# Two-layer hybrid trunk: one PSUM pool, FFN norm inside the first up product, operands in two passes, the attention's end reordered

## The chip, the cores and the metric

The kernel runs on one core of a Trainium2 chip. Its engines are TensorE (PE, with its weight loads as PEld), VectorE (DVE), ScalarE (ACT), GpSimd (POOL) and SyncE (SP, which issues most DMAs). The metric is device time in microseconds, lower is better. PSUM has eight banks of 128 x 512 float32, into which PE writes and from which DVE and ACT read.

## The reference

The model is a trunk of two pre-norm layers over 16 meta tokens and 512 tokens, width 1024. Layer 0 mixes tokens by causal pooling over windows of 2, 4, 8 and 16, layer 1 by stick-breaking attention with 16 heads of 64. A dense SwiGLU FFN with 2816 hidden units follows each, and a final RMSNorm stands at the end; only the 512 tokens are put out.

```python
def rmsnorm(x, g):
    y = xf * lax.rsqrt(jnp.mean(xf * xf, axis=-1, keepdims=True) + EPS)
    return (y * g.astype(jnp.float32)).astype(x.dtype)

def swiglu(h, w_gate, w_up, w_down):
    return (jax.nn.silu(h @ w_gate) * (h @ w_up)) @ w_down

def _sb_attend(qs, qpos, kvs, kpos):
    z = jnp.einsum('bqhd,bkhd->bhqk', q, k).astype(jnp.float32) * (HEAD_DIM ** -0.5)
    log_keep = jnp.where(mask, jax.nn.log_sigmoid(-z), 0.0)
    later = lax.cumsum(log_keep, axis=3, reverse=True) - log_keep
    a = jnp.where(mask, jnp.exp(jax.nn.log_sigmoid(z) + later), 0.0)
    return jnp.einsum('bhqk,bkhd->bqhd', a.astype(v.dtype), v)
```

## The kernel before

The residual stream lies transposed in SBUF as eight chunks `h0` to `h7` of 128 channels by 528 positions (`hT`). Every float32 product is made of three products of split numbers (`mm3`): high by high, low by high, high by low. ACT writes the high part (a cast), DVE the low part (a subtraction); `wsplit` (L92, L97) does so for weights, whose raw tiles come by DMA on SP's queue.

`Norm.chunk` is run on each chunk of the residual once it is final. It writes the chunk times the gain, split (`uh`, `ul`, L152 and L153), squares it (L157) and adds it to a running sum (L161; the last chunk's add is L128). The products start from these unscaled operands. `norm_bcast` later multiplies the sum by a matrix of ones on PE (L173: `fb0p`, `fb1p` for the FFNs, `abp` for the attention), and ACT and DVE make 1/rms of it (`rstd_of`, L135 to L139), by which the products' results are scaled (L364, L519).

An FFN has 22 hidden blocks of 128, in rounds of 2 and then 4. The first three (`plain`) take 24 products each for gate and up (48 in the first FFN, which works on two halves of 264). The other 19 (`strassen`) make gate and up of both halves of the positions in seven products of 12 steps each; for these `operands` builds seven split operands `xh`, `xl` of four slots each, in four passes of one slot: two scaled chunks `xn` (L381), four differences (L387), seven casts (L389) and seven subtractions (L390), all 264 or 256 wide. It runs after block 0, when 1/rms is there. Three accumulators `pa`, `pb`, `pc` hold the seven products; ACT copies parts of them (L412) and DVE combines them (L430 to L436). While a round's blocks are computed, the down products of the round before (`pd`, L304 and L337) run between them. In the second FFN the down products go to `hn`, with the positions on the partitions.

The attention works on eight pairs of heads. For a pair, `proj` makes q, k and v (`pj`), `Scores` the scores in three groups (`z_832`, `z_0`, `z_416`), each read by ACT as two sigmoids (`kp`, `sg`, L576). Then DVE runs a scan over `kp` (L581) and multiplies `sg` by it (L583), once per head. `turned` transposes the weights on PE (`t`, L594 and L607) and splits them (`a1..h`, `a1..l`, L614 and L616; `a`, L619), and `attend` multiplies them with v (`po`, L633). Output products `wo` (`pw`) of the pairs 0 and 1, 2 to 4, and 5 to 7 add into the residual (L660), in eight steps of six, nine and nine products. Those of 2 to 4 are spread over the last two pairs as filling; those of 5 to 7 end the attention.

A scheduler orders the instructions of each engine from the program, and `tc.issue_after` puts an instruction behind a marked one. In the attention `begin` uses it for the three groups and the steps between them; other steps are placed freely. PSUM is divided anew in each stage by `phase` (L63): `ps0` with eight banks for the pooling, `ps1` with six and two for the first FFN, `ps2` with four and two double ones for the attention, `ps3` as `ps1`. A pool is closed before the next opens. The lines given are those of the kernel before.

## Time and profile before

| what | value |
|---|---|
| runs | 1235.87, 1058.43, 1060.87 us; median 1060.87 |
| profiled execution | 1062.8 us, span 1061.0 us, mean granted clock 0.985 |
| PE busy | 1023.1 us (96%) |
| DVE busy | 856.6 us (81%) |
| ACT busy | 556.9 us (52%) |

The program has these stages, in us of the span: pooling to 37, first FFN 39 to 408, attention 408 to 691, second FFN 695 to 1053, and the last store. A row of the timeline gives start, length, engine, line, operation, output and inputs with buffer numbers left out, shape, and in brackets the idle time before it and what ended it. An overlap of pipelined products makes a row longer than the distance from one start to the next; that distance is what a product takes. A granted clock of 0.5 is TensorE at half speed.

### The profile page before, as it was taken

How to read it: one execution, taken by the hardware profiler on the slowest of the kernel's cores; microseconds unless marked ns; L12 is line 12 of the kernel's file. 1: busy time of each engine (PE TensorE's matmuls, PEld its weight loads, DVE VectorE, ACT ScalarE, POOL GpSimd, SP SyncE). 2: the span in 40 equal slices, each digit the busy share in tenths (PEclk: the TensorE clock that was granted, in tenths of full speed). 3: DMA queues.
4: the chain of work that ended last, by engine and by line, in shares of the span. 5: the costliest groups of instructions: out<-in, count | busy, mean ns of one | idle time of the engine just before them, and what ended most of it. 6: DMA issues, size and time to landing. Idle time of an engine off the chain costs nothing.

```text
span 1061.0 us, 18586 instructions
## 1 busy us (share of the span) xinstructions
PE 1023.1 (96%) x7302; PEld 949.3 (89%) x7302; DVE 856.6 (81%) x1529; ACT 556.9 (52%) x1131; POOL 6.2 (1%) x16
## 2 busy tenths in 40 slices
PE   8998999999999999999999998989999999999997
PEld 6997999999999998998888886867899999999985
DVE  7899987888878777678888987779977877788755
ACT  7555645454444455455555454555655444455544
POOL 1000000000000010000000000000000000000000
PEclk9999999999999999999999998989999999999999
DMA  9212323333333332211111211211223223333302
GB/s 351 72 51 69 128 94 100 101 100 100 100 100 100 99 120 82 78 40 61 40 51 37 69 58 66 80 62 58 100 100 115 84 100 99 100 100 120 109 31 80
DMA packets 43112, 95.73 MB, mean 90 GB/s; under 512 B 3328, under 2 KB 20096, under 8 KB 43024
## 3 DMA queue, kind: packets, MB, share of 16 engines
q1 hardware_dynamic: 42272, 93.40, 26.2%
q8 instruction: 57, 0.93, 0.3%
q10 hardware_dynamic: 752, 1.14, 0.3%
q14 instruction: 31, 0.25, 0.1%
HBM read 92.43 MB, written 2.10 MB: 89 GB/s over the span
## 4 chain that ended last, share of the span: by engine, by line
PE 78%; DVE 17%; issue 2%; ACT 1%; DMA 1%; SPq 0%; ACTq 0%; DVEq 0%
PE pb L106 15%; PE pd L106 11%; PE pd L331 11%; PE pa L106 10%; PE pc L106 10%; PE pj L106 9%; PE pp L106 4%; DVE kp L581 2%; PE pw L106 2%; PE z L567 2%; DVE xl L390 1%; DVE a L619 1%; PE t L594 1%; DVE t L387 1%; DVE sg L583 1%
## 5 line engine op out<-in xcount | busy, mean ns | idle before, releaser
L304 DVE TENSOR_TENSOR h<-pd,h 128x264 f32<-128x264 f32 x96 | 40.9, 427 | 14.0 <-PE pd L106 14.0
L92 ACT CAST ws_3h<-rgate 128x512 fp32r<-128x512 f32 x38 | 23.6, 620 | 53.3 <-PE pb L106 47.8
L581 DVE TENSOR_TENSOR_SCAN kp<-kp,estrip 128x1344 f32<-128x1344 f32 x16 | 47.3, 2954 | 3.8 <-ACT kp L576 3.4
L92 ACT CAST ws_4h<-s 128x512 fp32r<-128x512 f32 x38 | 23.6, 621 | 46.6 <-PE pa L106 27.7
L92 ACT CAST ws_5h<-s 128x512 fp32r<-128x512 f32 x38 | 23.6, 621 | 45.8 <-PE pb L106 34.7
L433 DVE TENSOR_TENSOR u<-pb,m 128x264 f32<-128x264 f32 (+1 forms) x38 | 16.3, 428 | 38.6 <-PE pb L106 38.6
L106 PE MATMUL pa<-xl,ws_0h 128*128 128x264 f32 (+1 forms) x152 | 43.3, 285 | 3.1 <-DVE xl L390 3.0
L106 PE MATMUL pb<-xl,ws_1h 128*128 128x264 f32 (+1 forms) x152 | 43.3, 285 | 1.0 <-DVE xl L390 1.0
L106 PE MATMUL pc<-xl,ws_2h 128*128 128x264 f32 (+1 forms) x152 | 43.1, 283 | 0.9 <-DVE xl L390 0.9
L106 PE MATMUL pb<-xh,ws_1h 128*128 128x264 f32 (+1 forms) x152 | 43.6, 287 | 0.2 <-ACT xh L389 0.2
L106 PE MATMUL pa<-xh,ws_3h 128*128 128x264 f32 (+1 forms) x152 | 43.6, 287 | 0.0
L106 PE MATMUL pa<-xl,ws_3h 128*128 128x264 f32 (+1 forms) x152 | 43.5, 286 | 0.0
L106 PE MATMUL pa<-xh,ws_3l 128*128 128x264 f32 (+1 forms) x152 | 43.3, 285 | 0.0
L106 PE MATMUL pc<-xh,ws_2l 128*128 128x264 f32 (+1 forms) x152 | 43.2, 284 | 0.0
L106 PE MATMUL pa<-xh,ws_0h 128*128 128x264 f32 (+1 forms) x152 | 43.1, 284 | 0.0
L106 PE MATMUL pb<-xh,ws_6l 128*128 128x264 f32 (+1 forms) x152 | 43.0, 283 | 0.0
L106 PE MATMUL pa<-xh,ws_0l 128*128 128x264 f32 (+1 forms) x152 | 43.0, 283 | 0.0
L106 PE MATMUL pb<-xh,ws_4l 128*128 128x264 f32 (+1 forms) x152 | 43.0, 283 | 0.0
L106 PE MATMUL pc<-xl,ws_5h 128*128 128x264 f32 (+1 forms) x152 | 42.9, 283 | 0.0
L106 PE MATMUL pb<-xh,ws_1l 128*128 128x264 f32 (+1 forms) x152 | 42.9, 283 | 0.0
L106 PE MATMUL pb<-xl,ws_4h 128*128 128x264 f32 (+1 forms) x152 | 42.9, 282 | 0.0
L106 PE MATMUL pc<-xh,ws_5h 128*128 128x264 f32 (+1 forms) x152 | 42.9, 282 | 0.0
(1179 smaller groups left out, 4110.9 us busy)
## 6 DMA issues: line engine op xcount, KB each, us to landing
rgate<-in_ffn_w_gate_dram SPq DMA_DIRECT2D x44, 512.0 KB, 3.5
rup<-in_ffn_w_up_dram SPq DMA_DIRECT2D x44, 512.0 KB, 3.5
rd<-in_ffn_w_down_dram SPq DMA_DIRECT2D x42, 512.0 KB, 3.6
rq<-in_sb_w_qkv_dram SPq DMA_DIRECT2D x8, 512.0 KB, 3.5
rk<-in_sb_w_qkv_dram SPq DMA_DIRECT2D x8, 512.0 KB, 3.4
rv<-in_sb_w_qkv_dram SPq DMA_DIRECT2D x8, 512.0 KB, 3.4
rwo<-in_sb_w_o_dram SPq DMA_DIRECT2D x8, 384.0 KB, 3.0
h<-in_x_t_dram SPq DMA_DIRECT2D x8, 264.0 KB, 6.9
```

Source lines behind the costliest of these rows:

```text
L92: nc.scalar.copy(hi, v[:, j:j + w])
L106: last = nc.tensor.matmul(o, lhsT=w, rhs=xx[:, sl], start=start and i == 0, stop=stop and i == 2, skip_group_check=more)
L304: nc.vector.tensor_tensor(out=hv, in0=pd, in1=hv, op=ALU.add)
L331: nc.tensor.matmul(pd, lhsT=hid[j][x_][:, ts], rhs=w_[:, sl], start=r > 0 and i + j == 0, stop=j == len(hid) - 1 and i == 2, skip_group_ch ...
L387: nc.vector.tensor_tensor(out=o, in0=a, in1=b, op=ALU.subtract)
L390: nc.vector.tensor_tensor(out=xl[i][:, m, :], in0=o, in1=f32(xh[i][:, m, :]), op=ALU.subtract)
L433: tt(out=u[:, a], in0=pb, in1=m1, op=ALU.add)
L567: nc.tensor.matmul(tz[:, hd, c:c + k1 - k0], lhsT=qq[hs, i * P:(i + 1) * P], rhs=kk[hs, k0:k1], start=j == 0 and c == 0, stop=False, skip_ ...
L581: nc.vector.tensor_tensor_scan(kp[:, hd, ::-1], kp[:, hd, ::-1], estrip[:, ::-1], 1.0, op0=ALU.mult, op1=ALU.max)
L583: return nc.vector.tensor_tensor(out=sg[:, hd, 0:STRIP - 1], in0=sg[:, hd, 0:STRIP - 1], in1=kp[:, hd, 1:STRIP], op=ALU.mult).ins
L594: nc.tensor.transpose(o, sg[:, c0:c0 + n], ident)
L619: nc.vector.scalar_tensor_tensor(a0[r, i], f32(a0h[r]), lo_rows[r], p2[r, 256:384], op0=ALU.mult, op1=ALU.add)
```

## The change

PSUM becomes one pool for the whole kernel: two double banks (`two`) and two banks each of `c` and `d`. `ps` hands out `one` as c and d in turn, `any` over all eight; `ps_pair` gives the plain blocks theirs. No pool closes any more. In the blocks of Strassen's scheme `pa` and `pb` share one double bank (`pab`), and their copies share tiles `ma`, `mb`.

The ones product of an FFN's norm stands inside block 0's up product, behind its fifth of eight steps (`FB = 4`), and the weights of blocks 1 and 2 are split behind the norm's sum and behind 1/rms. `operands` takes two passes of two slots, so that its differences, casts and subtractions are twice as wide; DVE has 44 instructions fewer in the program and ACT 28. Silu is taken in place.

In the attention every PE step goes through `queued`, which puts it behind the step before. Ahead of the last pair's scores no output product stands; one lies between its groups and three behind them. At the end, `begun` and `ended` divide each output step of the pairs 5 to 7: the products of pairs 5 and 6 of chunk c+1 stand ahead of that of pair 7 of chunk c, and the norm's chunk work follows each.

```diff
+FB = 4
...
-    @contextmanager
-    def phase(name, **bufs):
-        with tc.tile_pool(name=name, bufs=1, space=bass.MemoryType.PSUM) as pool:
-            psum["pool"], psum["bufs"] = pool, bufs
-            yield
+    psum = ctx.enter_context(tc.tile_pool(name="psum", bufs=1, space=bass.MemoryType.PSUM))
+    turn = {"one": 0, "any": 0, "pair": 0}
 
     def ps(name, tag, banks=1):
 
+        i = turn.get(tag, 0)
+        turn[tag] = i + 1
+        if tag == "any":
+            if i % 8 in (0, 1, 4, 5):
+                if i % 2 == 0:
+                    turn["tile"] = ps(name, "two", 2)
+                return turn["tile"][:, i % 2]
+            tag = "cd"[i % 2]
+        if tag == "one":
+            tag = "cd"[i % 2]
         shape = [P, 512] if banks == 1 else [P, banks, 512]
-        return psum["pool"].tile(shape, F32, tag=tag, name=name, bufs=psum["bufs"][tag])
+        return psum.tile(shape, F32, tag=tag, name=name, bufs=2)
+    def ps_pair(name):
+        i = turn["pair"]
+        turn["pair"] = i + 1
+        if i % 3 == 2:
+            return [ps(f"{name}{j}", "c") for j in range(2)]
+        pt = ps(name, "two", 2)
+        return [pt[:, 0], pt[:, 1]]
...
-                add_eps(self.acc, sq, self.acc)
+                self.done = add_eps(self.acc, sq, self.acc)
...
-                parts = [wsplit(raw_gu(kind, f), f"w{kind}{f}") for kind in ("gate", "up")]
-                g, sg, u = (gw(f"{i}{f}") for i in ("g", "sg", "u"))
-                for dst, (wh, wl) in zip((g, u), parts):
-                    pts = [ps(f"pp{f}", "w")[:, :sl.stop - sl.start] for sl in pieces]
+                parts = []
+                for kind in ("gate", "up"):
+                    with tc.issue_after(norm.done if f == 1 else fst[1]) if f else nullcontext():
+                        parts.append(wsplit(raw_gu(kind, f), f"w{kind}{f}"))
+                g, u = (gw(f"{i}{f}") for i in "gu")
+                prods = []
+                both = ps_pair(f"pp{f}") if not full else None
+                for i, (dst, (wh, wl)) in enumerate(zip((g, u), parts)):
+                    pts = [t[:, :sl.stop - sl.start] for t, sl in
+                           zip(ps_pair(f"pp{f}") if full else both[i:i + 1], pieces)]
+                    prods.append((dst, pts))
+                    mark = None
                     for k in range(KC):
-                        mm3([(t, slice(t0 + sl.start, t0 + sl.stop)) for t, sl in zip(pts, pieces)], wh[k], wl[k],
-                            uh[k], ul[k], k == 0, k == KC - 1)
-                    if not fst:
-                        fst.extend((norm_bcast([acc], f"fb{layer}", "d"), last_rstd[0]))
+                        with tc.issue_after(mark) if mark else nullcontext():
+                            last = mm3([(t, slice(t0 + sl.start, t0 + sl.stop)) for t, sl in zip(pts, pieces)], wh[k],
+                                       wl[k], uh[k], ul[k], k == 0, k == KC - 1)
+                        if i == 1 and k == FB and not fst:
+                            with tc.issue_after(last):
+                                fst.extend((norm_bcast([acc], f"fb{layer}", "d"), last_rstd[0]))
+                            mark = last_bcast[0]
...
-                for m in range(4):
+                for m in (0, 2):
                     xn = []
                     for c in (m, m + 4):
-                        t = fp.tile([P, L], F32, tag="xn", name=f"xn{c}", bufs=2)
-                        gc = gains[:, gcol + c:gcol + c + 1]
-                        nc.vector.scalar_tensor_tensor(t[:, tok], hT[c][:, tok], gc, rb[:, tok], op0=ALU.mult,
-                                                       op1=ALU.mult)
+                        t = fp.tile([P, 2, L], F32, tag="xn", name=f"xn{c}", bufs=2)
+                        for j in range(2):
+                            gc = gains[:, gcol + c + j:gcol + c + j + 1]
+                            nc.vector.scalar_tensor_tensor(t[:, j, tok], hT[c + j][:, tok], gc, rb[:, tok],
+                                                           op0=ALU.mult, op1=ALU.mult)
                         xn.append(t)
-                    b11, b12, b21, b22 = [t[:, s] for t in xn for s in halves]
+                    b11, b12, b21, b22 = [t[:, :, s] for t in xn for s in halves]
                     t1, t2, t3, t4 = [wk(f"t{i}") for i in range(4)]
                     for o, a, b in ((t1, b12, b11), (t2, b22, t1), (t3, b22, b12), (t4, b21, t2)):
                         nc.vector.tensor_tensor(out=o, in0=a, in1=b, op=ALU.subtract)
                     for i, o in enumerate((b11, t2, t1, b21, t3, b22, t4)):
-                        nc.scalar.copy(xh[i][:, m, :], o)
-                        nc.vector.tensor_tensor(out=xl[i][:, m, :], in0=o, in1=f32(xh[i][:, m, :]), op=ALU.subtract)
+                        hi, lo = xh[i][:, m:m + 2, :], xl[i][:, m:m + 2, :]
+                        nc.scalar.copy(hi, o)
+                        nc.vector.tensor_tensor(out=lo, in0=o, in1=f32(hi), op=ALU.subtract)
...
-                pa, pb, pc = [ps(f"p{i}{f}", "w")[:, :n] for i in "abc"]
+                pab = ps(f"pab{f}", "two", 2)
+                pa, pb, pc = pab[:, 0, :n], pab[:, 1, :n], ps(f"pc{f}", "c")[:, :n]
...
+                ma, mb = wk(f"ma{f}"), wk(f"mb{f}")
+                m1, m6, m5, m67 = ma[:, 0], ma[:, 1], mb[:, 0], mb[:, 1]
...
-    with phase("ps1", w=6, d=2):
-        ffn(0, 16, norm, before_attention)
-    with tc.tile_pool(name="att", bufs=1) as ap, phase("ps2", one=4, two=2):
...
+        pos = []
+        def queue():
+            return tc.issue_after(pos[0]) if pos else nullcontext()
+        def queued(*steps):
+            for st in steps:
+                with queue():
+                    pos[:] = [st()]
...
-            mark = None
-            for st in before:
-                mark = st()
-            with tc.issue_after(mark) if mark else nullcontext():
-                sc.group(0)
-                mark = sc.group(1)
-            for st in between:
-                with tc.issue_after(mark):
-                    mark = st()
-            with tc.issue_after(mark):
-                sc.group(2)
+            queued(*before, lambda: (sc.group(0), sc.group(1))[1], *between, lambda: sc.group(2))
...
-                fill = w[0:1], w[1:2], w[2:4]
+                fill = [], w[0:1], w[1:4]
...
-            for st in fill[2]:
-                st()
-            attend(p, 1, w1, v, of)
+            queued(*fill[2], lambda: attend(p, 1, w1, v, of))
             if p in (4, 5):
-                for st in early[4 * (p - 4):4 * (p - 3)]:
-                    st()
+                queued(*early[4 * (p - 4):4 * (p - 3)])
...
-        for c, st in enumerate(wo(5, NP)):
-            st()
+        raw, part = [], {}
+        def begun(c):
+            if c % 2 == 0:
+                raw[:] = [wraw(w_o[0, 5 * P:NP * P, c * P:(c + 2) * P].rearrange("(k p) f -> p k f", p=P), f"rwo5_{c}")]
+            ws = wsplit(raw[0][:, :, (c % 2) * P:(c % 2 + 1) * P], f"wo5_{c}")
+            pj = ps(f"pw5_{c}", "one")
+            part[c] = pj, ws
+            for j in range(2):
+                last = mm3([(pj, slice(0, SEQ))], ws[0][j], ws[1][j], *osp[5 + j], j == 0, False)
+            return last
+        def ended(c):
+            pj, ws = part[c]
+            last = mm3([(pj, slice(0, SEQ))], ws[0][2], ws[1][2], *osp[7], False, True)
+            nc.vector.tensor_tensor(out=hT[c][:, TOK], in0=pj, in1=hT[c][:, TOK], op=ALU.add)
             norms[1].chunk(c)
+            return last
+        queued(lambda: begun(0))
+        for c in range(KC):
+            queued(*([lambda: begun(c + 1)] if c + 1 < KC else []), lambda: ended(c))
...
-    ctx.enter_context(phase("ps3", w=6, d=2))
```

PE's queue at the last pair's scores (`z`, with `pw` the output products, `consts`, `qk` and `masks` inputs). Before, from the end of the first output product on:

```order
L106 MATMUL pw_0_8080<-os4h,wo_0l_8077 128x512
L567 MATMUL z_832_8091<-qk_1h,qk_0h 128x512 x2
L567 MATMUL z_832_8091<-qk_1l,qk_0h 128x512 x2
L567 MATMUL z_832_8091<-qk_1h,qk_0l 128x512 x2
...
L106 MATMUL pw_3_8178<-os2h,wo_3h_8174 128x512
L106 MATMUL pw_3_8178<-os2l,wo_3h_8174 128x512
L106 MATMUL pw_3_8178<-os2h,wo_3l_8175 128x512
L567 MATMUL z_416_8136<-qk_1h,qk_0h 128x400 x2
L567 MATMUL z_416_8136<-qk_1h,qk_0h 128x16 x2
```

After, at the same place, and where the third group stands:

```order
L569 MATMUL pv_7870<-consts,vm_7875 128x128
L598 MATMUL z_832_7927<-qk_1h,qk_0h 128x512 x2
L598 MATMUL z_832_7927<-qk_1l,qk_0h 128x512 x2
L598 MATMUL z_832_7927<-qk_1h,qk_0l 128x512 x2
...
L125 MATMUL pw_0_7963<-os2h,wo_0h_7959 128x512
L125 MATMUL pw_0_7963<-os2l,wo_0h_7959 128x512
...
L125 MATMUL pw_0_7963<-os4h,wo_0l_7960 128x512
L598 MATMUL z_416_7974<-qk_1h,qk_0h 128x400 x2
L598 MATMUL z_416_7974<-qk_1h,qk_0h 128x16 x2
...
L125 MATMUL pw_1_7999<-os2h,wo_1h_7995 128x512
L125 MATMUL pw_1_7999<-os2l,wo_1h_7995 128x512
```

The output product pw_0 stood ahead of the scores and now stands between their groups, and pw_1 to pw_3 stand behind the third group, where pw_1, pw_2 and a part of pw_3 stood ahead of it.

PE's queue at the entry of the second FFN (`pw_4` and the like are output products, `pp` the first gate and up products, `f1uh` and `f1ul` the norm's chunks). Before:

```order
L106 MATMUL pw_7_8528<-os7h,wo_7h_8524 128x512
L106 MATMUL pw_7_8528<-os7l,wo_7h_8524 128x512
L106 MATMUL pw_7_8528<-os7h,wo_7l_8525 128x512
L106 MATMUL pp_8591<-f1uh_8380,wgate0h_8570 128x512
L106 MATMUL pp_8591<-f1ul_8381,wgate0h_8570 128x512
L106 MATMUL pp_8591<-f1uh_8380,wgate0l_8571 128x512
L106 MATMUL pp_8591<-f1uh_8401,wgate0h_8570 128x512
```

After, in the middle of the output products, and further on at the norm's ones product:

```order
L125 MATMUL pw_3_8278<-os7h,wo_3l_8275 128x512
L125 MATMUL pp_8439<-f1uh_8244,wgate0h_8419 128x512
L125 MATMUL pp_8439<-f1ul_8245,wgate0h_8419 128x512
L125 MATMUL pp_8439<-f1uh_8244,wgate0l_8420 128x512
L125 MATMUL pw_5_8324<-os5h,wo_5h_8320 128x512
...
L125 MATMUL pp_8439<-f1uh_8335,wup0l_8434 128x512
L192 MATMUL fb1p_8479<-f1sq_8248,ones 128x264
L192 MATMUL fb1p_8481<-f1sq_8248,ones 128x264
L125 MATMUL pp_8439<-f1uh_8359,wup0h_8433 128x512
```

The first pp product followed the last output product; now pp products stand between the output products, and the ones product `fb1p` stands inside the up product.

DVE's queue among the operands of the second FFN (`t` differences, `xl` low parts, `ws` weights). Before:

```order
L387 TENSOR_TENSOR t_8665<-xn_8661 128x256
L97 TENSOR_TENSOR wd_0_0l_8930<-rd_0_0_8927,wd_0_0h_8929 128x512
L390 TENSOR_TENSOR xl_8561<-xn_8661,xh_8554 128x256
L390 TENSOR_TENSOR xl_8564<-xn_8663,xh_8557 128x256
L390 TENSOR_TENSOR xl_8566<-xn_8663,xh_8559 128x256
L400 TENSOR_TENSOR s_8996<-rgate_3_8989,s_8994 128x512
L364 TENSOR_TENSOR g_8785<-pp_8788,fb1r 128x512
```

After:

```order
L370 TENSOR_TENSOR hl_8640<-u_8585,hh_8639 128x512
L414 SCALAR_TENSOR_TENSOR xn_8539<-h_75,gains,fb1r 128x512
L414 SCALAR_TENSOR_TENSOR xn_8539<-h_76,gains,fb1r 128x512
L434 TENSOR_TENSOR s_8937<-rgate_4_8931,rup_4_8933 128x512
L424 TENSOR_TENSOR xl_8416<-t_8517,xh_8409 128x2x256
L420 TENSOR_TENSOR t_8542<-xn_8536 128x2x256
L424 TENSOR_TENSOR xl_8410<-xn_8536,xh_8403 128x2x256
L399 TENSOR_TENSOR u_8664<-g_8663,u_8664 128x512
```

The steps are twice as wide (128x2x256), and the second pass's `xl_8410` stands behind the low half of block 1's hidden units, `hl_8640`.

73 lines of the change are left out of this document (36 added, 37 removed).

## The prediction

> **What bounds the kernel now.** The page first: busy shares, then the engines' shares of the chain that ended last.
>
> ```profile
> PE 1023.1 (96%) x7302; PEld 949.3 (89%) x7302; DVE 856.6 (81%) x1529; ACT 556.9 (52%) x1131; POOL 6.2 (1%) x16
> PE 78%; DVE 17%; issue 2%; ACT 1%; DMA 1%; SPq 0%; ACTq 0%; DVEq 0%
> ```
>
> TensorE is the bound, and what a change of order can win is only the time in which it waits or runs at half clock. The second view splits the span by stage (stretch, its length, busy time of PE, PEld, DVE, ACT, POOL, granted clock, DMA share, GB/s).
>
> ```profile
> 39.00:104.00 65.00, 60.49 (x448) 58.26 (x449) 61.92 (x132) 35.01 (x78) 0.00 (x0) 0.95 0.18 60
> 104.00:400.00 296.00, 296.00 (x2433) 296.00 (x2432) 240.19 (x453) 149.84 (x300) 3.27 (x10) 1.00 0.32 106
> 640.00:660.00 20.00, 15.84 (x93) 12.51 (x92) 14.45 (x16) 9.49 (x18) 0.00 (x0) 0.92 0.20 67
> 690.60:705.50 14.90, 10.75 (x35) 8.31 (x34) 11.23 (x19) 6.10 (x10) 0.00 (x0) 0.77 0.21 70
> 705.50:760.00 54.50, 51.92 (x282) 44.35 (x281) 51.15 (x106) 32.63 (x70) 0.00 (x0) 0.97 0.19 68
> 760.00:1040.00 280.00, 280.00 (x1938) 260.39 (x1938) 215.43 (x383) 141.10 (x288) 0.00 (x0) 1.00 0.29 95
> ```
>
> The two long FFN stretches (576 us) have PE full at full clock: nothing to win there, only to lose. The loss sits at the seams, and the waits of PE name it (what waits, for what: total, times, longest):
>
> ```profile
> PE pp L106 <- DVE h L660: 4.1, 1, 4.1
> PE t L594 <- DVE sg L583: 3.6, 1, 3.6
> PE pa L106 <- DVE xl L390: 3.0, 3, 2.1
> PE pp L106 <- DVE h L266: 2.2, 1, 2.2
> PE z L567 <- ACT qk_1h L527: 1.6, 1, 1.6
> PE pb L106 <- DVE xl L390: 1.0, 1, 1.0
> PE pc L106 <- DVE xl L390: 0.9, 1, 0.9
> ```
>
> The first is the entry into FFN1, where the new PSUM pool opens only when the last residual add has read the old one; the second the last pair's scores; the fourth the entry into FFN0; the xl rows are the FFNs' operands. Granted clock adds to them: 0.95 of 65 us loses 3.3 us in FFN0's first stretch, 0.77 of 14.9 us loses 3.4 at FFN1's entry.
>
> **The last scores.** Timeline around them (start, length, engine, line, operation):
>
> ```profile
> 641.05 1.23 DVE L616 TENSOR_TENSOR a161l<-t,a161h 128x1024 fp32r<-128x1024 f32 x1
> 642.33 0.50 PE L567 MATMUL z<-qk_1h,qk_0h 64*128 64x512 f32 x2 [0.57 <-DVE a161l L616]
> 649.63 0.46 PE L567 MATMUL z<-qk_1h,qk_0h 64*128 64x400 f32 x4
> 651.83 2.96 DVE L581 TENSOR_TENSOR_SCAN kp<-kp,estrip 128x1344 f32<-128x1344 f32 x1 [1.64 <-ACT kp L576]
> 655.76 1.55 DVE L583 TENSOR_TENSOR sg<-sg,kp 128x1343 f32<-128x1343 f32 x1
> 657.45 2.36 PE L594 MATMUL t<-consts,sg 128*128 128x128 f32 x10 [3.59 <-DVE sg L583]
> 660.89 0.63 PE L106 MATMUL pw<-os3h,wo_4h 128*128 128x512 f32 x1
> 661.32 0.63 PE L106 MATMUL pw<-os3l,wo_4h 128*128 128x512 f32 x1
> 690.39 0.39 PE L106 MATMUL pw<-os7l,wo_7h 128*128 128x512 f32 x1
> 690.62 0.40 PE L106 MATMUL pw<-os7h,wo_7l 128*128 128x512 f32 x1
> ```
>
> A 512-wide product takes 0.23 us from start to start at full clock (the last two rows) and 0.43 after the 3.6 us wait (the two before). The order before has pw_0 ahead of the groups z_832 and z_0, and 21 products between z_0 and z_416; after, pw_0 alone lies between them. PE reached z_832 at 642.33 - 0.57 = 641.76. Without pw_0 (9 x 0.23 = 2.1) it comes at 639.7, but z_832 still takes the bank that a161l reads until 642.3: the wait grows from 0.57 to 2.6, since the transposes ahead of a161l stand where they stood. The saving starts behind it: z_416 comes 21 - 9 = 12 products, 2.8 us earlier, and with it the scan (649.0) and the step L583 (653.0, done 654.5). PE has all of its work done by 653.86 + 2.1 = 656.0 (it was idle 3.59 before 657.45), so the transposes no longer wait and start 1.5 us earlier. Behind them, DVE's second scan, L583, and the split of the weights set po_170, and at the pair's end I get 2.2 us. Against it stands the 2.6 us wait in front: FFN0's first stretch lost 3.3 us of clock (the 0.95 above) behind two waits of about that size, the entry's 2.2 and the 2.1 for xl, so some 1.7 each; here it would fall on the scores and pw_0, and delay the chain that has just been shortened. So from 2.2 (no clock lost) to -1.2 (as long a stretch as after the 3.6 us wait, 3.4 us lost); I take **+1.2**, between the two nearer cases.
>
> The Trainium skill (TensorE: Matmul & The Clock Gate, Part 1: The HAM clock gate) says that the clock goes to half after at least one idle window of about 3.4 us. By that rule a 2.6 us wait would cost no clock and the term would be 2.2; the trace disagrees, with the clock lost behind waits of 2.2 and 2.1 us.
>
> **The entry into FFN1.**
>
> ```profile
> 694.33 0.68 DVE L660 TENSOR_TENSOR h<-pw,h 128x512 f32<-128x512 f32 x1
> 695.16 0.77 PE L106 MATMUL pp<-f1uh,wgate0h 128*128 128x512 f32 x1 [4.15 <-DVE h L660]
> 705.60 0.61 PE L173 MATMUL fb1p<-f1sq,ones 128*128 128x264 f32 x2
> 708.29 0.71 DVE L136 TENSOR_TENSOR fb1t<-fb1r 128x528 f32<-128x528 f32 x1 [2.30 <-ACT fb1r L135]
> ```
>
> The pool's close goes, so the first pp products need only their own chunk. Since chunk c's third part now follows the first two of c+1, the adds spread: chunk 0's add can start 12 + 3 products (3.5 us) into the stage instead of behind 24 + 6, and the other seven follow every nine products (2.1 us). Between two adds DVE has at most three other steps of 0.6 to 0.7 us, so it keeps up, and the last chunk is added near 692, its low half and the sum of squares near 695. PE meanwhile has the pp products between the output products, then 32 more ahead of fb1p, which it reaches near 699: nobody waits. Gone are 4.15 us of wait and, at half clock, 14 products (from 695.16 on) of 0.43 instead of 0.23, 2.7 us: **+6.8**, from 4 (clock only partly back) to 7.5.
>
> **The FFNs' operands.** Each of four passes had 256-wide steps, now two passes with 512-wide ones.
>
> ```profile
> 720.56 0.42 DVE L387 TENSOR_TENSOR t<-xn,xn 128x256 f32<-128x256 f32 x1
> 720.89 0.68 DVE L350 TENSOR_TENSOR hl<-u,hh 128x512 fp32r<-128x512 f32 x1
> 721.50 0.41 DVE L390 TENSOR_TENSOR xl<-t,xh 128x256 fp32r<-128x256 f32 x1
> 748.38 0.75 DVE L390 TENSOR_TENSOR xl<-t,xh 128x256 fp32r<-128x256 f32 x2
> ```
>
> From start to start the narrow one takes 0.33 and the wide one 0.61, so a merger saves 0.05, and 22 of them 1.1 us of the 40.8 that DVE is busy from 708.29 to 749.1. With fb1p 6.6 earlier DVE starts at 701.7 and ends near 741.4, 7.7 earlier. PE, though, comes some 9 us earlier (6.8, the 2.2 above, and the products that now lie ahead of fb1p shorten what is left before pab), and what it needs comes in larger lumps: before, the first quarter of the operands was done after one narrow pass; now the second half of all seven starts 26 us behind the norm. Counting 0.6 us for each DVE row in its new order, hl of f=1 is written at 730.5, when PE would be there at 727.7; the second pass's xl0 at 734.3, against 731.5; xl1 at 740.9, against 739.9. That is 6.6 us, and with smaller ones 7.6, against the 4.2 that the stretch 705.5 to 760 loses now (2.6 not busy, 0.03 of 54.5 in clock): **-3.0** here, from 0 to -4.5.
>
> FFN0 has the same, with its entry.
>
> ```profile
> 47.92 0.71 DVE L128 SCALAR_TENSOR_TENSOR f0sq<-f0sq,f0sq 128x528 f32<-128x528 f32 x1
> 97.20 1.11 DVE L390 TENSOR_TENSOR xl<-t,xh 128x264 fp32r<-128x264 f32 x3
> ```
>
> The pool's close (2.2) and its share of lost clock (1.7) go, 3.9 us of PE. But DVE is the limit there: from the norm's sum (48.6) to the last xl (98.3) it has its list, which can start at most some 2.6 earlier and is 1.1 shorter, while the lumps cost about what they cost in FFN1, and xl waits of 2 us stood there already. I take **-1.0**, from -3 to +2.5.
>
> **FFN0's end.** The first pj (24 products) now runs between the last down products.
>
> ```profile
> 408.26 0.43 DVE L304 TENSOR_TENSOR h<-pd,h 128x264 f32<-128x264 f32 x1
> 411.18 0.70 DVE L128 SCALAR_TENSOR_TENSOR ansq<-ansq,ansq 128x528 f32<-128x528 f32 x1
> 414.47 1.05 PE L173 MATMUL abp<-ansq,ones 128*128 128x264 f32 x4
> ```
>
> Before, the norm's sum (411.9) was hidden behind all of pj_00, and abp came at 414.47. Now 18 of its products (4.2 us) come ahead of the last down product, so the last h is added at 412.4 and the sum, 3.6 later, at 416.1: abp is **1.6 later**, and so is the chain to the scores, which PE waits for already (the 1.6 us row of qk_1h); from 0 to -2.5.
>
> **No change:** in the saturated FFN stretches and the pairs 0 to 5 the products are the same, and the pairs' order too; silu in place and fewer buffers change no step's length. The cover is 576 us of full PE; if it is gone, see the second rival. From -1 to +1.
>
> **Sum.** 1.2 + 6.8 - 3.0 - 1.0 - 1.6 = 2.4 us. The profiled execution took 1062.8 (span 1061.0): 1060.4 after. The median of the runs is 1060.87, 0.18% under it, which gives **1058**.
>
> **Rivals.** First, the seams simply close: DVE's lists get their new start passed on, the lumps cost nothing, and the last scores lose no clock. That is 2.2 + 6.8 + 2.5 = 11.5 us, 1051 by the profile and 1049 as a median. For it: the waits are plain in the list; against it: DVE is busy 61.9 of 65 us in FFN0's first stretch, so that time gained by PE is waited for again. 0.25.
> Second, slower: pab is one tile of two banks, so a product into one half now also waits for the copy (ACT) out of the other. 113 such waits stand in the new order; most have 3.3 us of PE work as cover, as before, but a dozen have 1.4 to 1.95. A copy has to wait for the product, for ACT's current step of 0.6 and to run for 0.4: about 1.3. If ACT is a step or two late, each of the dozen costs up to 1 us: +12, 1072 by the profile, 1070 as a median. It decides where ACT is behind by more than 0.5 us; ACT is busy about half the time, so 0.12.
> Third, the change doesn't do what it says: the first pp of FFN1 finds its bank held by an output product all the same (the rotation gives it a bank that the last adds read), and 6.8 goes: 1065. The new order places pp between output products, which speaks against it. 0.08.
> The forecast's own case keeps 0.55.
>
> **Range and chances.** The case's own ends are about 1051 (all terms good) and 1068 (all bad); with the first rival below and most of the second left out, 1047 to 1068 holds 8 in 10. A measurement of this kernel tells 2%, 21 us, from no change: faster by that would need every wait at every seam to go, with the clock: 0.03. Slower by it needs the second rival at twice its price: 0.04. Within: 0.93.
>
> **What would show it.** In the changed profile: no wait of PE for h at either entry; the wait for sg gone and one of 2 to 3 us for a161l at the last scores, with or without slow products behind it; FFN1's fb1p near 699 on the old scale; waits for xl and hl of together over 6 us behind it; abp some 1.6 later. Wrong would be waits of pab for ACT copies in the full stretches, or operand waits no longer than before.

## The result and the profile after

The changed kernel took 1071.03 us as a median of four executions (1069.48 to 1072.49), the kernel before 1060.67 beside it (median of three, 1058.43 its lowest): a ratio of 1.0104, 95% interval 1.0080 to 1.0128. A fourth execution of the kernel before, 1235.87 us, fell in the chip's slow state and is left out. Timed once more later, the changed kernel took 1068.55 against 1060.33, 1.0089 [1.0065, 1.0114]. By the bound of 2% that is no change; by its interval it is about 1% slower, where the forecast was 1058 and its range ended at 1068.

Two profiled executions of the changed kernel are used below: one of 1071.04 us (span 1069.3, granted clock 0.979), "the first trace", and one with a span of 1066.8 us and clock 0.983, "the second". They are of the same program, and they differ by 2.5 us; where that comes from is itself one of the findings. Lines of the kernel after are numbered differently: L125 is before's L106 (products), L351 the second FFN's down products, L369 and L370 their operands hh and hl, L424 the low operands xl, L268 the pooling, L598 the scores, L703 the add into h. In kernels that differ in one part they lie a few lines off (L120 for L125, L187 for L192).

Busy time and the chain that ended last, first trace:

```profile
PE 1026.9 (96%) x7302; PEld 950.8 (89%) x7302; DVE 857.8 (80%) x1485; ACT 551.0 (52%) x1103; POOL 7.2 (1%) x16
PE 77%; DVE 17%; ACT 3%; issue 2%; DMA 1%; SPq 0%; DVEq 0%; ACTq 0%
```

The same 7302 products, 3.8 us more busy, which goes with the lower granted clock (0.979 against 0.985). DVE has its 44 instructions fewer and is as busy as before (857.8 against 856.6 us): the merger did not shorten its work, and the prediction had put no more than 0.05 us on a merged step. ACT's share of the chain went from 1 to 3%, which points at a new place where a cast ends last. PE's waits, first trace (what waits, for what: total, times, longest):

```profile
PE pab L125 <- DVE xl L424: 4.8, 2, 2.6
PE pool L268 <- DVE pl L275: 3.3, 2, 2.7
PE z L598 <- DVE a161l L659: 2.7, 1, 2.7
PE pd L351 <- ACT hh L369: 2.6, 1, 2.6
PE pd L351 <- DVE hl L370: 2.6, 1, 2.6
PE pw L125 <- DVE of L679: 2.1, 2, 1.1
```

Gone are the two waits of the entries (4.1 and 2.2) and the one for sg (3.6). Of those in the list, xl, a161l and hl had been worked out. Two large ones had not: the pooling's wait for pl, right at the start, and the one for hh, right at the end. The windows tell where the clock went (stretch, length, busy PE, PEld, DVE, ACT, POOL, granted clock, DMA share, GB/s), first trace:

```profile
0.00:39.00 39.00, 32.91 (x215) 27.39 (x216) 28.64 (x61) 21.07 (x39) 2.95 (x6) 0.96 0.70 253
39.00:104.00 65.00, 58.39 (x424) 55.84 (x423) 62.19 (x113) 36.76 (x66) 0.00 (x0) 0.89 0.19 61
104.00:380.00 276.00, 276.00 (x2268) 276.00 (x2268) 223.41 (x421) 134.87 (x284) 0.00 (x0) 1.00 0.31 102
700.00:765.00 65.00, 59.14 (x307) 49.90 (x306) 58.14 (x97) 36.32 (x65) 0.00 (x0) 0.92 0.22 70
765.00:1030.00 265.00, 265.00 (x1844) 246.68 (x1843) 210.47 (x372) 135.64 (x277) 0.00 (x0) 1.00 0.31 101
1040.00:1069.30 29.30, 20.19 (x98) 16.61 (x96) 16.13 (x45) 12.15 (x30) 0.00 (x0) 0.88 0.19 72
```

The long stretches are as full as before, so the second rival (products into pab waiting for copies of its other half) did not come: 276.00 of 276 and 265.00 of 265 us are busy. What was lost lies at the seams. To sum them, the same points of the work are found in both traces. Rows of before that the prediction does not show (the last is the last Strassen product, used further down):

```profile
407.86 0.28 PE L106 MATMUL pd<-hh,wd_7l 128*128 128x264 f32 x1
673.89 0.39 PE L633 MATMUL po<-a,vv 128*128 128x512 f32 x1
1035.18 0.28 PE L106 MATMUL pb<-xh,ws_6l 128*128 128x256 f32 x1
```

and the rows of the first trace that answer to them and to the prediction's (the last down product of FFN0, abp, the last pair's scores, the last product with v, fb1p):

```profile
417.18 0.28 PE L125 MATMUL pd<-hh,wd_7l 128*128 128x264 f32 x1
421.66 1.96 PE L192 MATMUL abp<-ansq,ones 128*128 128x264 f32 x4
649.14 0.76 PE L598 MATMUL z<-qk_1h,qk_0h 64*128 64x512 f32 x2 [2.67 <-DVE a161l L659]
681.45 0.39 PE L676 MATMUL po<-a,vv 128*128 128x512 f32 x1
708.84 1.05 PE L192 MATMUL fb1p<-f1sq,ones 128*128 128x264 f32 x4
```

- To the end of FFN0: 417.18 - 407.86 = 9.3, of which 4.2 are the 18 products of pj that now come earlier: **5.1 lost** (in the second trace 3.9).
- From there to abp: 421.66 - 414.47 = 7.2, so **2.1 lost** more.
- To the last pair's scores: 649.14 - 642.33 = 6.8, 0.4 regained.
- Scores to the last product with v: 32.3 now (681.45 - 649.14), 31.6 before (673.89 - 642.33): **0.7 lost**.
- From there to fb1p: 27.4 now and 31.7 before, and ten products (2.3 us) more are done in it: **6.6 won**.
- From fb1p to the last Strassen product: 334.9 now (1043.70 - 708.84; the row of 1043.70 is shown further down), 329.6 before, with three products (0.7 us) more in it: **4.6 lost**, at the operands.
- From there to the end: 25.6 now and 25.8 before, but 13 products (3.0 us) fewer are left for it: **2.8 lost**, the tail.

### The profile page after: what moved, and what is told of

It is laid out like the page before. It is cut to its first block, busy times and chain, and to the rows that moved or that the text cites. A ratio compares the mean times of both kernels' runs of the same rounds, so it can differ in the third digit from the quotient of the medians.

```text
span 1069.3 us, 18523 instructions
## 1 busy us (share of the span) xinstructions
PE 1026.9 (96%) x7302; PEld 950.8 (89%) x7302; DVE 857.8 (80%) x1485; ACT 551.0 (52%) x1103; POOL 7.2 (1%) x16
## 4 chain that ended last, share of the span: by engine, by line
PE 77%; DVE 17%; ACT 3%; issue 2%; DMA 1%; SPq 0%; DVEq 0%; ACTq 0%
PE pab L125 26%; PE pd L125 11%; PE pd L351 11%; PE pc L125 10%; PE pj L125 9%; DVE kp L612 2%; PE z L598 2%; PE pw L125 2%; PE pp L125 1%; DVE a L662 1%; DVE xl L424 1%; DVE sg L614 1%; PE mix L125 1%; DVE xn L414 1%; DVE of L679 1%
## 5 line engine op out<-in xcount | busy, mean ns | idle before, releaser
L125 PE MATMUL pab<-xl,ws_0h 128*128 128x264 f32 (+1 forms) x152 | 43.7, 288 | 4.8 <-DVE xl L424 4.8
L125 PE MATMUL pc<-xh,ws_2h 128*128 128x264 f32 (+1 forms) x152 | 43.3, 285 | 1.1 <-DVE u L396 1.1
L125 PE MATMUL pab<-xh,ws_0h 128*128 128x264 f32 (+1 forms) x152 | 43.4, 285 | 1.0 <-ACT xh L423 1.0
L125 PE MATMUL pc<-xl,ws_2h 128*128 128x264 f32 (+1 forms) x152 | 43.3, 285 | 1.0 <-DVE xl L424 1.0
L125 PE MATMUL pab<-xh,ws_0l 128*128 128x264 f32 (+1 forms) x152 | 43.7, 287 | 0.0
L125 PE MATMUL pc<-xh,ws_2l 128*128 128x264 f32 (+1 forms) x152 | 43.4, 286 | 0.0
L125 PE MATMUL pab<-xh,ws_1h 128*128 128x264 f32 (+1 forms) x152 | 43.4, 286 | 0.0
L125 PE MATMUL pab<-xl,ws_1h 128*128 128x264 f32 (+1 forms) x152 | 43.3, 285 | 0.0
L125 PE MATMUL pab<-xh,ws_1l 128*128 128x264 f32 (+1 forms) x152 | 43.2, 284 | 0.0
L125 PE MATMUL pab<-xh,ws_6l 128*128 128x264 f32 (+1 forms) x152 | 43.1, 283 | 0.0
L125 PE MATMUL pc<-xh,ws_5h 128*128 128x264 f32 (+1 forms) x152 | 43.0, 283 | 0.0
L125 PE MATMUL pab<-xh,ws_4l 128*128 128x264 f32 (+1 forms) x152 | 43.0, 283 | 0.0
L125 PE MATMUL pab<-xl,ws_3h 128*128 128x264 f32 (+1 forms) x152 | 43.0, 283 | 0.0
L125 PE MATMUL pc<-xl,ws_5h 128*128 128x264 f32 (+1 forms) x152 | 43.0, 283 | 0.0
L125 PE MATMUL pab<-xh,ws_3l 128*128 128x264 f32 (+1 forms) x152 | 42.9, 282 | 0.0
L125 PE MATMUL pab<-xl,ws_6h 128*128 128x264 f32 (+1 forms) x152 | 42.9, 282 | 0.0
L125 PE MATMUL pab<-xl,ws_4h 128*128 128x264 f32 (+1 forms) x152 | 42.9, 282 | 0.0
```

The lines of the kernel that those rows point to most:

```text
L125: last = nc.tensor.matmul(o, lhsT=w, rhs=xx[:, sl], start=start and i == 0, stop=stop and i == 2, skip_group_check=more)
```

## The experiments

The theory after this comparison: three edits that had not been costed, or not by enough, lost what the entry won: the pooling in shared double banks, the empty place ahead of the last scores, and the order of the last down products. The rival: the merged operands and the shared pab cost it, spread over both FFNs. Each experiment alters the changed kernel.

**The tail held back.** The down products of the last round's second position block are put behind the last product of the last Strassen block, so that they lie under the chain that makes hh.

```diff
-                        mm3([(o, slice(0, n))], w[0][k], w[1][k], xh[i][:, k, :], xl[i][:, k, :],
-                            start and k == 0, k == 3, not start)
+                        lastprod[:] = [mm3([(o, slice(0, n))], w[0][k], w[1][k], xh[i][:, k, :], xl[i][:, k, :],
+                                           start and k == 0, k == 3, not start)]
...
-                    down_n(r, t, e, prev, ws[e], "dc"[e], sl)
+                    with tc.issue_after(lastprod[0]) if t == 1 else nullcontext():
+                        down_n(r, t, e, prev, ws[e], "dc"[e], sl)
```

> The changed kernel with one edit: the down products of the second position block of the last round are held behind the last product of the last FFN block. Theory (TensorE ran out of filling at the end, since with four open accumulators instead of eight all of their products had been used up ahead of the last block's end): the 2.6 us wait for hh near 1044 goes, with the slow products behind it, and the span falls from 1069.3 to about 1065.2. Rival (the chain from the last product to hh became longer, since pa and pb are one tile, and the filling does not matter): the wait moves, at most 1 us is won, span 1068.3 or more.

Measured: 1064.75 us in one execution, its span of 1063.0 below the 1065.2 of the theory; the wait for hh is gone from its list. Of the gain, 1.9 us stand already at the first product of Strassen's scheme of this FFN (733.52 against 735.38), ahead of the edit, and so are not its work.

**The operands in four narrow passes again**, in both FFNs, as before (the tiles t1 to t4 get a tag of their own).

```diff
-                for m in (0, 2):
+                for m in range(4):
...
-                        t = fp.tile([P, 2, L], F32, tag="xn", name=f"xn{c}", bufs=2)
+                        t = fp.tile([P, L], F32, tag="xn", name=f"xn{c}", bufs=2)
...
-                        hi, lo = xh[i][:, m:m + 2, :], xl[i][:, m:m + 2, :]
+                        nc.scalar.copy(xh[i][:, m, :], o)
```

> The changed kernel with operands in four narrow passes again (two of the temporaries' tiles fewer than before the change). Theory (the lumps cost): the loss between 60 and 100 us falls from 11.4 us towards the 8.5 of before, that behind the second FFN's entry from 10.1 to 6 or 7; span about 1062 to 1063. Rival (DVE's lists set the end, not their grain): the merger's saved DVE time is lost and nothing won, span 1069 to 1071.

Measured: 1068.17 us. The second FFN got 2.6 of its loss back (from fb1p to the end 357.9 us, against 360.5), the first one nothing: its last down product comes at 418.06, against 417.18. Half of the expectation fell: by this one execution, what is lost in the first FFN isn't the width of its operands.

**The output products ahead of the last scores put back** (one group ahead, one between, two behind).

```diff
-                fill = [], w[0:1], w[1:4]
+                fill = w[0:1], w[1:2], w[2:4]
```

> The changed kernel with the output products around the last pair's scores placed as before. Theory (the new placing won nothing, since the wait for a161l in front took what the wait for sg behind gave): from the last pair's scores to the last po 31.6 us as before, against 32.3 after the change; span 1068.5. Rival (my prediction, the new placing is worth 1.2 to 2.2 us): span 1070.5 to 1071.5.

Measured: 1063.95 us, below both expectations: from the last scores to the last product with v it is 28.2 us, not the 31.6 of before.

**The pooling in a pool of its own**, with eight single banks as before; one pool for all the rest.

```diff
-            if i % 8 in (0, 1, 4, 5):
-                if i % 2 == 0:
-                    turn["tile"] = ps(name, "two", 2)
-                return turn["tile"][:, i % 2]
-            tag = "cd"[i % 2]
+            return psum["pool"].tile([P, 512], F32, tag="any", name=name, bufs=8)
...
+    psum["pool"] = ctx.enter_context(tc.tile_pool(name="psum", bufs=1, space=bass.MemoryType.PSUM))
     ffn(0, 16, norm, before_attention)
```

> The changed kernel with the pooling in a PSUM pool of its own with eight single banks, closed before the one pool for the rest opens. Theory (the shared double banks delay the pooling): the 2.7 us wait of pool for pl goes, the last mix comes at 36.6 instead of 39.8, and the first pp at 39.1 behind the close, 0.9 earlier; of this 0 to 1.7 us reaches the end, span 1067.6 to 1069.3. Rival (the pooling is later for another reason, as its DMAs or DVE's order): the last mix stays near 39.8, and the close adds its 2.2: span 1071.

Measured: 1063.73 us, much more than expected; fb0p starts at 47.98 where it stood at 51.73.

**All three together**: the tail held back, the products put back and the pooling's own pool in one kernel.

> The changed kernel with three edits together: the held down products at the end, the output products around the last scores as before, the pooling in a pool of its own. Theory (three separate losses at three places, which add up): against the changed kernel -3.1 to -4.4, -4.1 and -3.8, so a span of 1054 to 1056, a median near 1056.5 and a ratio of 0.995 to the kernel before. Rival (what is won early is waited for again later): a span of 1058 or more.

Measured: 1058.60 us, ratio 0.9988 [0.9974, 1.0003], 2.1 above the theory's 1056.5. The three single executions lie 6.3, 7.1 and 7.3 us under the changed kernel's median of 1071.03, 20.7 in all; together the edits gave about 12. Either they overlap or the comparison of single executions with that median flattered them. Two more edits were put on top of the three.

**The first pj behind the last down product**, as before:

```diff
-                    last = mm3([(pj, sl)], wh[k], wl[k], uh[k], ul[k], k == 0, k == KC - 1)
+                    with tc.issue_after(lastdown[0]) if not rbs else nullcontext():
+                        last = mm3([(pj, sl)], wh[k], wl[k], uh[k], ul[k], k == 0, k == KC - 1)
```

> The three edits, and the first pj of the attention held behind the last down product of the first FFN. Theory (the interleaving uncovers the last chunk's norm chain): from the last down product to the first scores 15.3 us as before the change, with all 24 products inside it, instead of 14.0 with 6, so 2 us less in all; span 2 us under that of the three edits. Rival (DVE's and ACT's chain to the scores is as long either way): no difference, within 0.7.

Measured: 1055.13 us, 0.9954 [0.9938, 0.9969], 3.5 under the three alone; the two intervals do not meet.

**Narrow operands in the second FFN alone** (the four narrow passes of above where the block is not the full first FFN):

```diff
+                if full:
...
+                else:
+                    for m in range(4):
```

> The three edits, and four narrow passes of operands in the second FFN alone. Theory (the lumps cost there): the loss from 705 to 760 falls from 10 us to 7 or 8, span 2 to 3 us under that of the three edits. Rival (DVE's whole list decides): no difference, or 1 us more.

Measured: 1055.81 us, 0.9966 [0.9946, 0.9986], 2.8 under the three alone. The two intervals overlap, but the traces agree with it: from fb1p to the end it is 353.5 us, against 356.2 in the three alone and 356.3 with the pj put back.

**One part kept alone: the pool without the division of the last output products.** The output steps of pairs 5 to 7 have nine products each again, queued.

```diff
+        for c, st in enumerate(wo(5, NP)):
+            queued(st)
+            norms[1].chunk(c)
```

> The changed kernel with the output steps of pairs 5 to 7 undivided, nine products in a row for each chunk. Theory (the one pool removed the entry's wait, since the first pp no longer needs the last add, and the division only covers os7): the last pair's os7 is waited for, 2 to 3 us, at the first output step, and fb1p is reached with little more loss; span 1071 to 1073. Rival (the division is what spreads the adds and removes the wait): a wait of 3 us or more for the norm's chunks returns at the entry, with slow products; span 1075.

Measured: 1069.12 us. The wait of 4.15 us at the entry does not come back. From the last product with v to fb1p it takes 28.8 us, 27.4 with the division, and one short wait of the first output product appears (pw for os7h, 1.1 us). So the division is not what removed the entry's wait: it is gone without it too, which leaves the single pool (no run closed a pool there again). The division was worth 1.4 us.

**All five edits in one kernel**, and then with the norm's ones product of the second FFN at the first step of the up product instead of the fifth.

> All five edits: held down products, output products as before, own pool for the pooling, the first pj held, narrow operands in the second FFN. Theory (the losses lie at separate places): the median of the three edits, 1058.6, less 3.5 for pj and 2.8 for the operands, 1052.3, ratio about 0.992 to the kernel before. Rival (one of the two was only a better clock stretch in that job): 1055, ratio 0.995.

```diff
-                        if i == 1 and k == FB and not fst:
+                        if i == 1 and k == (FB if full else 0) and not fst:
```

> The five edits, and the norm's ones product of the second FFN behind the first step of the up product instead of the fifth. Theory (after the entry DVE's operand list is what PE waits for, and it starts with the ones product, which comes some 4 us after its sum is ready): fb1p 2.8 us earlier, and as much won from 705 to 760: a median 2 to 2.8 us under that of the five edits. Rival (the waits there come from casts on ACT or from weights): less than 1 us.

Measured: all five 1052.57 us, 0.9936 [0.9918, 0.9954]; with the earlier ones product 1052.37 us, 0.9927 [0.9912, 0.9941]. Here the two kernels stand at fb1p and at the first product of Strassen's scheme, all five first:

```profile
696.67 1.05 PE L187 MATMUL fb1p<-f1sq,ones 128*128 128x264 f32 x4
723.22 0.28 PE L120 MATMUL pab<-xh,ws_0h 128*128 128x256 f32 x1
```

and with the earlier ones product:

```profile
695.07 1.05 PE L187 MATMUL fb1p<-f1sq,ones 128*128 128x264 f32 x4
724.89 0.28 PE L120 MATMUL pab<-xh,ws_0h 128*128 128x256 f32 x1
```

These two times can't be compared as they stand, since the second execution was later already ahead of the edit, at the last product with v:

```profile
669.29 0.39 PE L693 MATMUL po<-a,vv 128*128 128x512 f32 x1
670.89 0.40 PE L693 MATMUL po<-a,vv 128*128 128x512 f32 x1
```

Counted from there, fb1p comes 3.2 us earlier, with twelve products fewer ahead of it; the first product of Strassen's scheme comes no earlier (54.0 us against 53.9), and the end 1.3 us earlier (379.6 against 380.9). By the medians it is 0.2, with an uncertainty of some 2 us. So the expected 2 to 2.8 did not come, and whether there is a gain of about 1 is open. Both kernels are faster than the kernel before, by about 0.7%, which is clear of the noise but under the bound of 2%: that is the change without the parts that were found to lose; it keeps the single pool behind the pooling, the ones product inside the block, the divided output products and, in the first FFN, the wide operands.

**The single edits timed in rounds**: the changed kernel and the three kernels of above, unaltered, on one chip, to tell overlap from chance.

> The changed kernel itself, timed beside the three kernels with one part altered. Both theories: 1071 us, from 1069 to 1073, as its four runs so far (1069.48 to 1072.49).

> The kernel with only the final FFN's down products held back behind the last strassen product, timed in rounds (its single execution took 1064.75). Theory: its own worth is the 2.62 us wait for hh and, in some executions, one slow stretch of about 1.7 behind it, so 3 to 4.5 below the changed kernel, a median of 1067; the single one had in addition a slow stretch less in FFN0 by chance. Rival: the single execution is the typical one, 1064 to 1065, and the three parts overlap, since all three together gave 12.4 and the single ones add up to 20.7.

> The kernel with only the output products ahead of the last scores put back, in rounds (its single execution took 1063.95). Theory: its own worth is what lay between the last scores and the last po in the two traces, 32.3 against 28.2, so 4.1, a median of 1067; the rest of the single execution's gain was two slow stretches less, one in FFN0 and one at the tail (its tail had the same 2.62 us wait with no slow product behind it). Rival: the single one is typical, 1063 to 1064.5.

> The kernel with only the pooling stage in a pool of its own with eight single banks, in rounds (its single execution took 1063.73). Theory: its own worth is what stands at the first pa/pab, 78.47 against 74.61, so 3.9, a median of 1067; the rest was slow stretches less in FFN0 and at the tail. Rival: the single one is typical, 1063 to 1064.5.

| kernel | median us | ratio to before | under the changed kernel |
|---|---|---|---|
| changed | 1068.55 | 1.0089 [1.0065, 1.0114] | |
| tail held back | 1066.64 | 1.0063 [1.0048, 1.0078] | 1.9 |
| products ahead of the scores | 1066.26 | 1.0057 [1.0042, 1.0072] | 2.3 |
| pooling in its own pool | 1062.96 | 1.0030 [1.0016, 1.0044] | 5.6 |

They add up to 9.8 us; the three together had gained 1.0089 - 0.9988, 1% or 10.7 us. So nothing shows an overlap. Of the 10.9 us between 20.7 and 9.8, 7.4 come from the reference: the changed kernel's own median was 1071.03 then and is 1068.55 now, and it was used three times. Only some 3.5 come from the single executions, and they went both ways (1.9 and 2.3 us under their kernels' medians, and 0.8 above). The first two medians came out near what the theory of chance said, but at 1.9 the tail is below the 3 to 4.5 given for it and the fill below its 4.1, while the pooling's is above. With the intervals above, each of these differences is uncertain by some 3 us, so that of the three only the pooling's is clear of noise by its median alone; the traces tell the parts more closely, below.

## Why the prediction was wrong

**The entry into FFN1: right.** Forecast +6.8, measured +6.6. Before, from the last product with v to fb1p:

```profile
674.05:705.55 31.50, 27.35 (x106) 21.77 (x106) 22.40 (x36) 16.47 (x28) 0.00 (x0) 0.89 0.25 84
```

After, first trace:

```profile
681.60:708.80 27.20, 27.00 (x117) 21.60 (x116) 22.61 (x36) 17.59 (x29) 0.00 (x0) 1.00 0.23 78
```

Both halves of the term are there: PE idle 4.15 of 31.50 us became 0.2 of 27.20, and the clock went from 0.89 to 1.00, with some ten products more in the shorter time. The third rival (the bank still held) is out.

**FFN1's operands: right in kind, too small.** Forecast -3.0, from 0 to -4.5, with waits of 2.8 for hl, 2.8 for one xl and 1.0 for another. The first trace has the first two:

```profile
740.67 0.50 PE L351 MATMUL pd<-wd_0h,hl 128*128 128x512 f32 x1 [2.57 <-DVE hl L370]
744.41 0.58 PE L125 MATMUL pab<-xl,ws_0h 128*128 128x256 f32 x1 [2.25 <-DVE xl L424]
```

Together they are 4.8, under the 6 that the prediction gave as its sign. Measured is -4.6 (second trace -4.8), at the bad end of the range: the prediction counted waits alone, and in the 54.5 us from fb1p on the granted clock is 0.91 now, where it was 0.97. Narrow operands in this FFN alone gave 2.8 us of it back; what holds the rest was not separated.

**FFN0's end: right in kind, a little short.** Forecast -1.6, by the traces -2.1 and, second trace, -1.7; putting pj back gave 3.5 by the medians, which is more than the traces hold at that place. The nearest pair of traces agrees in its first product of Strassen's scheme to 0.01 us (pooling in its own pool, 74.69, and pj put back on top of the three, 74.68): abp comes at 415.60 and 414.34, the last scores at 643.26 and 641.14, so by it pj is worth 1.3 at abp and 2.1 at the scores.

**FFN0's start: the failing step.** The prediction took DVE's list to start 2.6 us earlier because the pool's close was gone, and put -1.0 on the operands. It put no cost on the stage ahead of it, although the change gives the pooling's products other banks, two of each four in a shared double bank. There, in the first trace:

```profile
19.81 0.39 PE L268 MATMUL pool<-band,ah 128*128 128x264 f32 x1 [2.71 <-DVE pl L275]
21.53 0.42 PE L268 MATMUL pool<-band,ah 128*128 128x264 f32 x1
21.75 0.42 PE L269 MATMUL pool<-band,al 128*128 128x264 f32 x1
```

and with the pooling's own pool, in the execution timed in rounds:

```profile
PE pool L265 <- DVE al L242: 1.6, 2, 0.9
0.00:39.00 39.00, 34.25 (x230) 27.98 (x231) 31.63 (x68) 26.11 (x49) 2.95 (x6) 1.00 0.71 254
74.69 0.28 PE L120 MATMUL pab<-xh,ws_0h 128*128 128x264 f32 x1
```

A pooling product finds its bank not yet read: the reader, pl on DVE, stands behind two splits of x, and PE waits 2.71 us; then come products 0.22 apart where 0.12 is full clock. With eight single banks the wait is the 0.9 of before, the granted clock of the stage 1.00 instead of 0.96. The second trace of the changed kernel has its first pab of FFN0 at:

```profile
78.80 0.28 PE L125 MATMUL pab<-xh,ws_0h 128*128 128x264 f32 x1
```

That is 4.1 later than 74.69, and it passes through to abp (420.09 against 415.60). Executions that share this part of the kernel differ here by up to some 1.5 us, but the two groups do not meet: this product starts at 78.2 to 79.4 in the eight traces with the shared banks and at 74.6 to 76.2 in the seven with the pooling's own pool. Set against the 3.9 that the changed kernel's second trace loses by FFN0's end, it is all of it: what the prediction did cost there comes out about even, not -1.0. Whether the shared reading of the two halves or the place of these banks in the rotation makes the wait was not separated.

**The last scores: the sign was wrong, the mechanism was named.** Forecast +1.2, between 2.2 with no clock lost and -1.2 with a long slow stretch; measured -0.7, near the lower end. Second trace of the changed kernel, from the wait to the third group:

```profile
648.10 0.50 PE L598 MATMUL z<-qk_1h,qk_0h 64*128 64x512 f32 x2 [2.67 <-DVE a161l L659]
652.54 0.63 PE L125 MATMUL pw<-os2h,wo_0l 128*128 128x512 f32 x1
652.96 0.63 PE L125 MATMUL pw<-os3h,wo_0h 128*128 128x512 f32 x1
655.61 0.47 PE L598 MATMUL z<-qk_1h,qk_0h 64*128 64x400 f32 x4
```

With one group put back ahead of the scores, in rounds:

```profile
648.11 0.50 PE L598 MATMUL z<-qk_1h,qk_0h 64*128 64x512 f32 x2 [0.57 <-DVE a161l L659]
651.12 0.39 PE L125 MATMUL pw<-os3h,wo_1h 128*128 128x512 f32 x1
651.35 0.40 PE L125 MATMUL pw<-os3l,wo_1h 128*128 128x512 f32 x1
652.61 0.46 PE L598 MATMUL z<-qk_1h,qk_0h 64*128 64x400 f32 x4
```

Both reach the scores within 0.01 us of each other: the group ahead only fills the wait for a161l. Both have nine output products between z_0 and z_416. All that differs is the clock: products 0.42 apart against 0.23, so that z_416, and the scan behind it, come 3.0 us later. That loss stands in the prediction's term as 1.7; it was 3.0. The last product with v then is 4.05 later (680.40 against 676.35). The empty place ahead of the scores was therefore a loss by itself; the fewer products behind it were the gain.

This pair is at one end of what the kept traces show. From the last scores to the last product with v it takes 32.3 us in six and 30.8 in two of the eight traces with the place empty, and 28.2 in three and 29.8 in four of the seven with the group put back; it was 31.6 in the one trace of before. So the term was -0.7 six times and +0.8 twice, and the group is worth 2.8 us on their average, near the 2.3 of the medians.

**"No change" at the tail: a failing step.** The term took the full stretches as cover and let the last products ride with them. Before, the last Strassen product (1035.18, shown above) had 28 down products behind it, 6.1 us up to 1041.40, under which hh was made. ACT's part of the chain, before:

```profile
1027.03 0.38 ACT L429 ACTIVATE sg<-pa 128x256 f32<-128x256 f32 x1
1036.75 0.62 ACT L349 CAST hh<-u 128x512 fp32r<-128x512 f32 x1 [0.70 <-DVE u L436]
```

After, first trace:

```profile
1043.70 0.28 PE L125 MATMUL pab<-xh,ws_6l 128*128 128x256 f32 x1
1043.82 0.63 PE L351 MATMUL pd<-wd_1l,hh 128*128 128x512 f32 x2
1044.48 0.38 ACT L461 ACTIVATE sg<-pab 128x256 f32<-128x256 f32 x1
1045.22 0.42 DVE L465 TENSOR_TENSOR u<-pab,ma 128x256 f32<-128x256 f32 x1
1046.40 0.62 ACT L369 CAST hh<-u 128x512 fp32r<-128x512 f32 x1 [1.54 <-DVE u L468]
1047.07 0.50 PE L351 MATMUL pd<-wd_0h,hh 128*128 128x512 f32 x1 [2.62 <-ACT hh L369]
1049.39 0.63 PE L351 MATMUL pd<-wd_0h,hl 128*128 128x512 f32 x1
1049.82 0.63 PE L351 MATMUL pd<-wd_0l,hh 128*128 128x512 f32 x1
```

Two products are left behind it; the others have been used up ahead of it or need hh themselves. The chain sg, u, hh is the work of ACT and DVE on one block, and PE waits 2.62 us for it. A likely reason why the products ran out stands in the kernels' text: the down products of the last round took their banks from the tags `d` and `w`, eight in all, and take them from `d` and `c` now, four in all (the last block's own accumulators are among them), so that fewer sums can be begun ahead of hh. No run varied that number; the wait stays at 2.6 with narrow operands, with undivided output products, with the pooling's own pool and with the group put back ahead of the scores.

The tail held back is a clean pair: in its execution in rounds the first pab of this FFN comes at 735.37, in the first trace of the changed kernel at 735.38, and the spans are 1064.8 and 1069.3. So holding the tail is worth 4.5 us there, 2.6 of wait and 1.8 of clock; against the second trace, whose products behind the same wait are not slow, it is 3.0. Median: 1.9. Not all of that had been lost by the change: measured against the kernel before, the tail cost 2.8 in the first trace and 1.1 in the second, so that the held order is better than that of before by 1.7 to 1.9.

The chain has also become longer. Before, the silu of pa (sg) started 8.2 us ahead of the last Strassen product and hh 1.6 behind it; now they start 0.8 and 2.7 behind it. It is so in every block: before, sg<-pa starts 5.2 to 8.3 us ahead of the block's last product in all 38 blocks, in both traces of the changed kernel sg<-pab starts 0.5 to 1.1 behind it in all 38. The silu stands at the same place in both programs, so that this fits pa and pb being one tile now, whose reader waits for the last product into either half; no run gave pa a tile of its own to show it. The second rival looked for products that wait for a copy out of the shared tile. What came is the reverse, a read that waits for products: in the full stretches it is covered, and at the tail it is about 1.1 of the 2.62 us (an estimate from 2.7 - 1.6).

**Sum.** By the first trace: -5.1 - 2.1 + 0.4 - 0.7 + 6.6 - 4.6 - 2.8 = -8.3; the span grew by 8.3 (1069.3 - 1061.0). Forecast: +2.4. Of the difference of 10.7 the pooling and FFN0 hold 4.1, the tail 2.8, the last scores 1.9, the operands 1.6, FFN0's end 0.5 and the entry 0.2; 0.4 were regained ahead of the last scores. So the steps that failed are two places at which the prediction put no cost, the banks of the pooling stage and the end of the last block, and one that it costed with the wrong sign, the last scores.

## What to carry to other kernels

List every stage whose buffers the change renames, not only those whose order it changes: here the loss of the pooling stage came from a bank assignment in a helper. An independent product is worth most under the last chain, and least ahead of it; before products are let free to move, ask which of them cover the end. Products that stand ahead of a wait which comes anyway cost nothing and may keep the clock; taking them out can lose more than the wait's length. Where two accumulators become one tile, look at the readers of each half as well as at the products into it.

## What the runs showed of the hardware

A wait of the same length at the same place is followed by half clock in one execution and not in another of the same program. In the first trace of the changed kernel the products behind the 2.62 us wait for hh are 0.43 apart from 1048.6 to 1052.0 (above). In the second, behind the same wait:

```profile
1046.22 0.50 PE L351 MATMUL pd<-wd_0h,hh 128*128 128x512 f32 x1 [2.62 <-ACT hh L369]
1048.17 0.39 PE L351 MATMUL pd<-wd_0h,hl 128*128 128x512 f32 x1
1048.40 0.40 PE L351 MATMUL pd<-wd_0l,hh 128*128 128x512 f32 x1
```

they are 0.23 apart, and that is about 1.7 us of the 2.5 between the two spans. So the prediction's price of "1.7 for a wait of some 2.6" is a chance and not a rate. From the wait for hh to the end it takes 22.2 us in three and 20.6 in five of the eight kept traces that have this wait, of the changed kernel and of its variants. Behind a161l's 2.67 us, the scan starts 9.7 us after the scores in six and 8.2 in two of eight; with the group put back it starts after 6.7, so that this wait cost 3.0 or 1.5 of clock.

The clock records of the traces show why these prices come in steps. In all sixteen kept traces every stretch at half clock between the start and the one that runs into the end is 3.41 us long or two, three or four times that, and 3.41 us at half clock lose 1.7. The first trace has twelve such lengths, the second ten and the kernel before eight. The Trainium skill (TensorE: Matmul & The Clock Gate, Part 1: The HAM clock gate) says that the activity window of about 3.4 us runs freely, so that the point of transition varies from run to run; the slow stretch from 1048.6 to 1052.0 is 3.4 long, and the others are whole multiples of that, which agrees. Its condition of at least one idle window for going to half clock does not agree: no wait of PE in these two traces is longer than 2.71 us.

It follows for the measuring that one execution of each kernel, set against a median of another time, could not price these edits: three single ones added up to 20.7 us, where the medians of one job gave 9.8 and the three together 10.7.
